# Alternating gate and recurrent projection tiles, one convolution tap a step, in a one-core decoder step

## The chip, the core and the metric

The kernel runs on one core of a Trainium2 chip. A core has a matrix engine (TensorE, here PE, with its weight load PEld), a vector engine (VectorE, here DVE), a scalar engine (ScalarE, here ACT), GpSimd (here POOL) and a queue engine (SyncE, here SP) that starts most DMAs. PE writes to PSUM, in eight banks; DVE and ACT read PSUM and SBUF. Each engine works off its own list of instructions in order, and waits on semaphores where it needs another engine's result. The metric is the device time of one execution in microseconds (us).

## The reference, cut to what matters

The reference is one layer of a decoder on 512 prompt positions and 8 x 4 sample positions (544 columns in all). All in float32.

```
h = RMSNorm_pre(x)
[x_r | q | k | v | g_A | g_B] = h @ W_in                # 1024 -> 4608
A: xc = conv4(x_r) + b;  r, i = sigmoid(block gates of xc)
   a = exp(-8 r softplus(-lam));  h_t = a h_(t-1) + sqrt(1 - a^2) * i * xc
B: attention over a window of 128 (8 query heads, 2 kv heads, sinks, relative bias)
m = (sigmoid(g_A) * (A @ W_A) + sigmoid(g_B) * (B @ W_B)) @ W_out
x = x + RMSNorm_post(m);  then a convolutional feed-forward (1024 -> 8192 -> 1024)
```

`conv4` is a causal convolution of width 4 along the positions, each channel by itself: four products with a scalar per channel, added up.

## The kernel before, in words

Channels lie on the 128 partitions and positions along the free dimension. To keep float32 accuracy, each operand of a matmul is split in a high part (rounded to fp32r, made by ACT with a Copy) and a low part (the rest, made by DVE with a subtraction, which reads the same source and the high part). A product is three matmuls: high by high, high by low, low by high.

**Steps.** The input projection is cut in tiles of 128 output columns. One tile is two calls of `step` (line 342), the first for columns 0 to 255 (matmuls with 256 columns), the second for columns 256 to 543 (288 columns); a step is 24 matmuls over eight blocks of 128 input channels. This text numbers the steps from 0. Steps 0 to 23 are q, k and v. Steps 24 to 39 are the eight tiles of the gate g_B (keys `("in", 28 + c)`, written to `ga`), steps 40 to 55 the eight recurrent tiles x_r (keys `("in", c)`, written to `xr`). Then come steps 56 to 71, the attention output projection (`ao`, matmuls `pmao`), the gate g_A, the recurrent output projection (`lo`) and `out`.

**Ticks.** After the matmuls of step s, `tick` (line 194) sets the clock `now` to s + 1 and writes the other engines' work of that tick in this order: the high parts of the weights of a later tile (ACT, line 281); the `done` function of step s - 1 (list `late`), which reads PSUM; the side jobs that are due (`sides`), in order of their due time; the list `after`; the low parts of the weights (DVE, line 288). So each tick's work stands in this order in the queues of ACT, DVE, POOL and PE, and a tick's work on an engine runs when that engine has come that far. The weights are split two tiles ahead (`look=2`), from step 50 one tile ahead (`look=1`).

**Side jobs.** `attn_unit` is one of 16 units of prompt attention (two heads by 128 positions), begun at the ticks in `ATTN` (8 to 45); each yield passes on to the next tick: scores `psc` on PE; softmax (`s`, `st`) on DVE and ACT; transposes `pt` on PE; split into `tH` (ACT) and `tL` (DVE); the product with V (`pvp`); for every second unit the split of two heads' results into `aH` (ACT, line 840) and `aL` (DVE, line 841). `sample_attn` does the sample positions in two groups (begun at ticks 38 and 43): its transposes `pst` are copied to `spt` by DVE (lines 902 and 903), multiplied in the same tick on PE (`pso`), copied (`so`), transposed (`psot`) and split for eight heads into `aH` (line 921) and `aL` (line 922), 16 columns each, all from one PSUM tile.

**The recurrent branch.** `xr_done` (line 929) scales the projection into the tile `xr`, POOL having written its three leading columns, and after the second half ACT makes the first tap, `xc = xr * w0 + b` (line 943). `xr_taps`, put on the list `after`, adds the other three taps on DVE: each is a scalar_tensor_tensor of 568 columns that reads `xr` and `xc` and writes `xc`. `gates`, due at the ticks in `GATES` (51, 53, 55 and 57 for the first four tiles), splits `xc` (`xcH` on ACT, `xcL` on DVE), multiplies by the block gates (`pg` on PE) a tick later, and takes two sigmoids (`rg`, `ig` on ACT) a tick after that. `lru_exp` (ticks 58 to 61 for the first four) takes tanh and exp on ACT and a square on POOL (line 988). `gate_later` takes the sigmoid of `ga` at ticks 52 to 59. The order of PE, ACT, DVE and POOL in this part is as written; nothing reorders it.

Of the kernel before, what the change touches and what calls it, by code (L numbers as in the profile page):

```python
# [14 lines left out]
ALU = mybir.AluOpType  # L15
# [5 lines left out]
SEQ = 512  # L21
# [8 lines left out]
NH = 8  # L30
# [5 lines left out]
FLAT = SEQ + 7 * DB  # L36
# [42 lines left out]
GATES = (51, 53, 55, 57, 73, 74, 75, 76)  # L79
# [44 lines left out]
def hawk_step(ctx, tc, I, O):  # L124
# [36 lines left out]
    def f32(ap):  # L161
        return ap.bitcast(F32)
# [4 lines left out]
    def sub(out, a, b):  # L167
        dve.tensor_tensor(out=out, in0=a, in1=b, op=ALU.subtract)  # L168
# [7 lines left out]
    def stt(out, a, s_, b, op0, op1):  # L176
        dve.scalar_tensor_tensor(out=out, in0=a, scalar=s_, in1=b, op0=op0, op1=op1)  # L177

    side, now, serial, late, last, mids, after = [], [0], [0], [], [], [], []

    def start_at(t, gen):
        serial[0] += 1
# [9 lines left out]
    def tick(target=0, dt=1):  # L194
        now[0] += dt
        todo = late[:]
        late.clear()
        split = [wsplit_hi(u) for u in wclaim(target)]
        parts_ = [sides, lambda: [f() for f in todo]]
        for f in parts_ if now[0] < TURNED else parts_[::-1]:  # L200
            f()
        for f in after:
            f()
        after.clear()
        for u in split:
            wsplit_lo(*u)
        for f in last:
            f()
        last.clear()
# [23 lines left out]

    qkv_order = (16, 18, 8, 9, 10, 11, 17, 19, 12, 13, 14, 15)
    order = [("in", c) for c in qkv_order]
    order += [("in", 28 + c) for c in range(8)]
    order += [("in", c) for c in range(5)] + [("wg", 0)] + [("in", c) for c in range(5, 8)]
    order += [("ao", c) for c in range(8)] + [("wg", 1)]
    order += [("in", 20 + c) for c in range(8)]
    order += [("lo", c) for c in range(8)]  # L240
# [549 lines left out]
    def attn_unit(hp, n):  # L790
        kv, np_ = hp // 2, n // 2
        nk = 1 if n == 0 else 2
        w = nk * P
        k0 = (n + 1) * P - w
        kh, kl = (K.t[kv][j][:, k0:k0 + w] for j in range(2))
        ps = PX(f"psc{hp}_{n}")
        for j in range(2):
            qh, ql = (Q.t[2 * hp + j][z][:, n * P:(n + 1) * P] for z in range(2))
            o = ps[:, j * w:(j + 1) * w]
            mm(o, qh, kh, True, False)  # L800
            mm(o, ql, kh, False, False)
            mm(o, qh, kl, False, True)
        yield
        s = T(f"s{hp}_{n}")
        s3 = s[:, 0:2 * w].rearrange("p (h j) -> p h j", h=2)
        stt(s3, ps[:, 0:2 * w].rearrange("p (h j) -> p h j", h=2), rq[:, n:n + 1], btab[hp][:, :, 2 * WIN - w:2 * WIN],
            ALU.mult, ALU.add)
        se = softmax_a(s3, 2, sinkb[:, 2 * hp:2 * hp + 2], f"{hp}_{n}")
        yield
        softmax_b(s3, 2, *se)  # L810
        yield
        pt = PX(f"pt{hp}_{n}")
        for ch in range(nk):
            for j in range(2):
                pe.transpose(pt[:, (2 * ch + j) * P:(2 * ch + j + 1) * P], s3[:, j, ch * P:(ch + 1) * P], ident)
        yield
        tH, tL = T(f"tH{hp}_{n}", F32R), T(f"tL{hp}_{n}", F32R)
        act.activation(tH[:, 0:2 * w], pt[:, 0:2 * w], AF.Copy)
        sub(tL[:, 0:2 * w], pt[:, 0:2 * w], f32(tH[:, 0:2 * w]))
        yield  # L820
        if n % 2 == 0:
            pvps[hp] = PX(f"pvp{hp}_{np_}")
        pvp = pvps[hp]
        o = pvp[:, (n % 2) * 256:(n % 2 + 1) * 256]
        for ch in range(nk):
            vh, vl = (V.t[kv][z][:, k0 + ch * P:k0 + (ch + 1) * P] for z in range(2))
            th, tl = (x[:, ch * 256:(ch + 1) * 256] for x in (tH, tL))
            mm(o, vh, th, ch == 0, False)
            mm(o, vl, th, False, False)
            mm(o, vh, tl, False, ch == nk - 1)  # L830
        if n % 2 == 1:
            yield
            for j in range(2):
                hd = 2 * hp + j
                if np_ == 0:
                    A.alloc(hd)
                src = pvp.rearrange("p (n h q) -> p n h q", n=2, h=2)[:, :, j, :]
                oh, ol = (A.get(hd, 0, z) if np_ == 0 else A.t[hd][z][:, 256:512] for z in range(2))
                oh, ol = (x.rearrange("p (n q) -> p n q", n=2) for x in (oh, ol))
                act.activation(oh, src, AF.Copy)  # L840
                sub(ol, src, f32(oh))


# [16 lines left out]
    def sample_attn(g):  # L860
# [54 lines left out]
        pe.transpose(px[:, 0:P], so, ident)  # L915
        yield
        ov = px[:, 0:P].rearrange("p (b h t) -> p b h t", b=4, h=NH)
        for hd in range(NH):
            oh, ol = (A.t[hd][z][:, SEQ + 16 * g:SEQ + 16 * g + 16].rearrange("p (b t) -> p b t", b=4)
                      for z in range(2))  # L920
            act.activation(oh, ov[:, :, hd, :], AF.Copy)
            sub(ol, ov[:, :, hd, :], f32(oh))


# [4 lines left out]
    def xr_done(c, a, ps):  # L929
        if a == 0:  # L930
            xr = xrt[c] = T(f"xr{c}")
            pool.memset(xr[:, 0:3], 0.0)
            pool.tensor_copy(xr[:, SEQ + 3:SEQ + 3 + 7 * DB].rearrange("p (b i) -> p b i", b=DB)[:, :, 0:3],
                             stT[:, c, 0:24].rearrange("p (b i) -> p b i", b=DB))
            scaled(xr[:, 3:259], ps, 0)
            return
        xr = xrt[c]
        smpv = xr[:, SEQ + 3:SEQ + 3 + 7 * DB].rearrange("p (b i) -> p b i", b=DB)
        mul(xr[:, 259:515], ps[:, 0:256], rep[:, 256:512])
        mul(smpv[:, :, 3:7], ps[:, 256:288].rearrange("p (b t) -> p b t", b=DB),  # L940
            rep[:, SEQ:NT].rearrange("p (b t) -> p b t", b=DB))
        xc[c] = S(f"xc{c}")
        act.activation(xc[c][:, 0:FLAT], xr[:, 0:FLAT], AF.Identity, bias=pv[:, C_B + c:C_B + c + 1],
                       scale=pv[:, C_W + c:C_W + c + 1])
        after.append(lambda: xr_taps(c))

    def xr_taps(c):
        xr = xrt[c]
        smpv = xr[:, SEQ + 3:SEQ + 3 + 7 * DB].rearrange("p (b i) -> p b i", b=DB)
        for t in range(1, 4):  # L950
            wv = pv[:, C_W + 8 * t + c:C_W + 8 * t + c + 1]
            stt(xc[c][:, 0:FLAT], xr[:, t:t + FLAT], wv, xc[c][:, 0:FLAT], ALU.mult, ALU.add)
        pool.tensor_copy(stage[:, c, 0:3], xr[:, SEQ:SEQ + 3])
        pool.tensor_copy(stage[:, c, 3:27].rearrange("p (b i) -> p b i", b=DB), smpv[:, :, 4:7])

# [129 lines left out]

    for c in range(8):
        for a in range(2):
            step(("in", 28 + c), h, a, gate_done(sg, c, "ga", True))
        start_at(GATES[0] + c + 1, once(gate_later, sg, c))
    for c in range(8):  # L1090
        for a in range(2):
            step(("in", c), h, a, lambda a, ps, c=c: xr_done(c, a, ps), look=1 if now[0] + 1 >= GATES[0] else 2)

# [874 lines left out]
```

## Time and profile before

| what | value |
|---|---|
| median of 3 runs | 1008.49 us (1007.88 to 1010.76) |
| the profiled execution | 1007.64 us, its span 1005.8 us |
| PE busy in the span | 984.9 us (98%) |
| DVE busy | 750.1 us (75%) |
| ACT busy | 567.8 us (56%) |
| POOL busy | 158.8 us (16%) |
| mean granted PE clock | 0.998 |

The profile is of one execution; its span runs from the first to the last instruction. Lines L12 are lines of the kernel printed above. A row of the timeline gives start, duration, engine, line, operation and the tiles it writes and reads; in brackets the time for which the engine had been idle just before, and the instruction on another engine that ended it. Buffer numbers are left out of the names, so that `xr` stands for all eight tiles.

### The profile page before, as it was taken

How to read it: one execution, taken by the hardware profiler on the slowest of the kernel's cores; microseconds unless marked ns; L12 is line 12 of the kernel's file. 1: busy time of each engine (PE TensorE's matmuls, PEld its weight loads, DVE VectorE, ACT ScalarE, POOL GpSimd, SP SyncE). 2: the span in 40 equal slices, each digit the busy share in tenths (PEclk: the TensorE clock that was granted, in tenths of full speed). 3: DMA queues.
4: the chain of work that ended last, by engine and by line, in shares of the span. 5: the costliest groups of instructions: out<-in, count | busy, mean ns of one | idle time of the engine just before them, and what ended most of it. 6: DMA issues, size and time to landing. Idle time of an engine off the chain costs nothing.

```text
span 1005.8 us, 20110 instructions
## 1 busy us (share of the span) xinstructions
PE 984.9 (98%) x7783; PEld 972.4 (97%) x7783; DVE 750.1 (75%) x1609; ACT 567.8 (56%) x1362; POOL 158.8 (16%) x269
## 2 busy tenths in 40 slices
PE   9999999888999999999999999999999999999997
PEld 8999999888999999999999999999999999999996
DVE  6776666876765854489787687878888888888765
ACT  6544334447749534456776656565656565656652
POOL 2143000000512543020000101111111111111004
PEclk9999999999999999999999999999999999999999
DMA  7665222321332354317235768585858586758612
GB/s 209 174 226 181 75 74 85 96 73 56 91 106 84 93 166 131 110 43 245 74 90 137 178 139 180 139 183 136 187 131 193 124 191 127 189 130 216 195 45 89
DMA packets 211000, 135.62 MB, mean 135 GB/s; under 512 B 8846, under 2 KB 197022, under 8 KB 210873
## 3 DMA queue, kind: packets, MB, share of 16 engines
q1 hardware_dynamic: 198920, 112.72, 39.5%
q0 software_dynamic: 11920, 19.59, 11.8%
q10 hardware_dynamic: 64, 2.04, 0.5%
q8 instruction: 61, 1.00, 0.4%
q14 instruction: 35, 0.28, 0.1%
HBM read 111.78 MB, written 11.37 MB: 122 GB/s over the span
## 4 chain that ended last, share of the span: by engine, by line
PE 88%; DVE 6%; ACT 4%; DMA 1%; issue 1%; SPq 0%; DVEq 0%; ACTq 0%
PE pmin L165 18%; PE pmdn L165 17%; PE pux L1517 15%; PE puy L1517 8%; PE pq L1517 6%; PE pmout L165 5%; PE pmlo L165 5%; PE puz L1517 4%; PE pmao L165 3%; DMA raw_in<-in_w_in_dram 1%; DVE xc L177 1%; PE psc L165 1%; PE pvp L165 1%; PE ptok L165 1%; PE pg L165 1%
## 5 line engine op out<-in xcount | busy, mean ns | idle before, releaser
L165 PE MATMUL pmin<-hH,wh_in 128*128 128x256 f32 (+1 forms) x568 | 165.1, 293 | 0.1
L165 PE MATMUL pmin<-hL,wh_in 128*128 128x256 f32 (+1 forms) x568 | 162.7, 289 | 0.0
L165 PE MATMUL pmin<-hH,wl_in 128*128 128x256 f32 (+1 forms) x568 | 158.9, 288 | 3.1 <-DVE wl_in L288 3.1
L165 PE MATMUL pmdn<-fH,wh_dn 128*128 128x256 f32 (+1 forms) x448 | 129.0, 288 | 0.2 <-DVE ft L174 0.2
L165 PE MATMUL pmdn<-fL,wh_dn 128*128 128x256 f32 (+1 forms) x448 | 128.9, 288 | 0.0
L165 PE MATMUL pmdn<-fH,wl_dn 128*128 128x256 f32 (+1 forms) x448 | 128.9, 288 | 0.0
L177 DVE SCALAR_TENSOR_TENSOR uc<-u,fv,uc 128x560 f32<-128x560 f32 x128 | 102.0, 797 | 13.3 <-ACT uc L1548 13.2
L165 PEld LDWEIGHTS pmin<-hH,wl_in 128*128 128x128 f32 x568 | 105.1, 188 | 3.7 <-DVE wl_in L288 3.5
L165 PEld LDWEIGHTS pmin<-hH,wh_in 128*128 128x128 f32 x568 | 106.9, 188 | 1.6 <-issue 1.2
L165 PEld LDWEIGHTS pmin<-hL,wh_in 128*128 128x128 f32 x568 | 107.1, 189 | 0.1
L165 PEld LDWEIGHTS pmdn<-fH,wh_dn 128*128 128x128 f32 x448 | 84.2, 188 | 0.6 <-issue 0.6
L165 PEld LDWEIGHTS pmdn<-fH,wl_dn 128*128 128x128 f32 x448 | 84.3, 188 | 0.0
L165 PEld LDWEIGHTS pmdn<-fL,wh_dn 128*128 128x128 f32 x448 | 84.2, 188 | 0.0
L1643 ACT COPY u<-pux 128x272 f32<-128x272 f32 x52 | 20.1, 387 | 83.3 <-PE pux L1517 83.3
L168 DVE TENSOR_TENSOR u<-puy,u 128x240 f32<-128x240 f32 (+2 forms) x78 | 24.7, 344 | 49.2 <-PE puy L1517 32.5
L174 DVE TENSOR_TENSOR ft<-ft,pmdn 128x256 f32<-128x256 f32 (+1 forms) x104 | 45.3, 436 | 17.0 <-PE pmdn L165 16.4
L281 ACT ACTIVATE wh_in<-raw_in 128x512 fp32r<-128x512 f32 x70 | 42.5, 626 | 26.8 <-issue 9.8
L1548 ACT ACTIVATE uc<-u,fv 128x560 f32<-128x560 f32 x64 | 48.2, 755 | 0.0
L288 DVE TENSOR_TENSOR wl_in<-raw_in,wh_in 128x512 fp32r<-128x512 f32 x70 | 47.1, 684 | 1.2 <-ACT wh_in L281 1.0
L165 PE MATMUL pmao<-aH,wl_ao 128*128 128x288 f32 (+1 forms) x128 | 37.4, 292 | 2.7 <-DVE wl_ao L288 2.7
L1443 POOL DMA_DIRECT2D raw_up_s<-raw_up_s x26 | 22.7, 872 | 101.5 <-DMA raw_up_s<-raw_up__7496 4.5
L168 DVE TENSOR_TENSOR wl_dn<-raw_dn,wh_dn 128x512 fp32r<-128x512 f32 x56 | 38.4, 686 | 0.0
(779 smaller groups left out, 3395.0 us busy)
## 6 DMA issues: line engine op xcount, KB each, us to landing
raw_in<-in_w_in_dram SPq DMA_DIRECT2D x35, 512.0 KB
raw_dn<-in_w_down_dram SPq DMA_DIRECT2D x56, 256.0 KB
raw_up_s<-in_w_up_dram SPq DMA_DIRECT2D x25, 512.0 KB
raw_up_s<-raw_up_s POOLq DMA_DIRECT2D x26, 256.0 KB, 5.6
raw_ao<-in_w_attn_o_dram SPq DMA_DIRECT2D x8, 512.0 KB
raw_lo<-in_w_lru_o_dram SPq DMA_DIRECT2D x8, 512.0 KB
raw_out<-in_w_out_dram SPq DMA_DIRECT2D x8, 512.0 KB
xdram<-xn POOLq DMA_DIRECT2D x8, 272.0 KB, 8.9
```

The costliest lines, as they stand in the source:

```text
L165: pe.matmul(out, l, r, start=start, stop=stop)
L168: dve.tensor_tensor(out=out, in0=a, in1=b, op=ALU.subtract)
L174: dve.tensor_tensor(out=out, in0=a, in1=b, op=ALU.add)
L177: dve.scalar_tensor_tensor(out=out, in0=a, scalar=s_, in1=b, op0=op0, op1=op1)
L281: act.activation(hl[0], raw, AF.Copy)
L288: (eng or dve).tensor_tensor(out=hl[1], in0=raw, in1=f32(hl[0]), op=ALU.subtract)
L1443: pool.dma_start(out=w["p4"], in_=w["p2"], accum_op=ALU.add)
L1517: pe.matmul(ps[:, :HN], w, x, start=start and k == 0 and i == 0, stop=stop and k == 3 and i == 2, skip_group_check=True)
L1548: act.activation(yt[j][:, 0:FLATU], u[:, 0:FLATU], AF.Copy, scale=fv[:, j:j + 1])
L1643: act.copy(e[nm_], z)
```

## The change

It has three parts.

First, the gate tiles and the recurrent tiles alternate: step 24 + 4c and the next are gate tile c, the two after these recurrent tile c. The order in which the weights are loaded (`order`) changes with it. The gate weights `wg` stay at the same place in it, after 13 tiles. The ticks of the side jobs are the same numbers as before.

Second, the three DVE taps of a recurrent tile are no longer written in one piece on `after`. They go on a list, `taps`, and each tick takes one from it, written directly behind the `done` functions, ahead of the side jobs. The second half of recurrent tile c comes to its `done` at tick 24 + 4c + 5, so its taps stand in the three ticks after that. Before, all three stood at the end of tick 43 + 2c.

Third, in `attn_unit` both high parts are written ahead of both low parts, and in `sample_attn` all eight high parts ahead of the eight low ones, which come one tick later.

```diff
@@ tick
         split = [wsplit_hi(u) for u in wclaim(target)]
-        parts_ = [sides, lambda: [f() for f in todo]]
+        tap = taps[:1]
+        parts_ = [sides, lambda: [f() for f in todo + tap]]
+        del taps[:1]
         for f in parts_ if now[0] < TURNED else parts_[::-1]:
@@ the order of the weights
-    order += [("in", 28 + c) for c in range(8)]
-    order += [("in", c) for c in range(5)] + [("wg", 0)] + [("in", c) for c in range(5, 8)]
+    pairs = [("in", z + c) for c in range(8) for z in (28, 0)]
+    order += pairs[:13] + [("wg", 0)] + pairs[13:]
@@ attn_unit
+            parts_ = []
             for j in range(2):
...
                 act.activation(oh, src, AF.Copy)
+                parts_.append((ol, src, oh))
+            for ol, src, oh in parts_:
                 sub(ol, src, f32(oh))
@@ sample_attn
-        for hd in range(NH):
-            oh, ol = (A.t[hd][z][:, SEQ + 16 * g:SEQ + 16 * g + 16].rearrange("p (b t) -> p b t", b=4)
-                      for z in range(2))
+        parts_ = [[A.t[hd][z][:, SEQ + 16 * g:SEQ + 16 * g + 16].rearrange("p (b t) -> p b t", b=4) for z in range(2)]
+                  for hd in range(NH)]
+        for hd, (oh, ol) in enumerate(parts_):
             act.activation(oh, ov[:, :, hd, :], AF.Copy)
+        yield
+        for hd, (oh, ol) in enumerate(parts_):
             sub(ol, ov[:, :, hd, :], f32(oh))
@@ xr_done and the taps
-        after.append(lambda: xr_taps(c))
+        taps.extend(lambda t=t: xr_tap(c, t) for t in range(1, 4))
 
-    def xr_taps(c):
+    def xr_tap(c, t):
         xr = xrt[c]
+        wv = pv[:, C_W + 8 * t + c:C_W + 8 * t + c + 1]
+        stt(xc[c][:, 0:FLAT], xr[:, t:t + FLAT], wv, xc[c][:, 0:FLAT], ALU.mult, ALU.add)
+        if t < 3:
+            return
         smpv = xr[:, SEQ + 3:SEQ + 3 + 7 * DB].rearrange("p (b i) -> p b i", b=DB)
-        for t in range(1, 4):
-            wv = pv[:, C_W + 8 * t + c:C_W + 8 * t + c + 1]
-            stt(xc[c][:, 0:FLAT], xr[:, t:t + FLAT], wv, xc[c][:, 0:FLAT], ALU.mult, ALU.add)
         pool.tensor_copy(stage[:, c, 0:3], xr[:, SEQ:SEQ + 3])
@@ the steps
     for c in range(8):
         for a in range(2):
-            step(("in", 28 + c), h, a, gate_done(sg, c, "ga", True))
+            step(("in", 28 + c), h, a, gate_done(sg, c, "ga", True), look=1 if now[0] + 1 >= GATES[0] else 2)
         start_at(GATES[0] + c + 1, once(gate_later, sg, c))
-    for c in range(8):
         for a in range(2):
             step(("in", c), h, a, lambda a, ps, c=c: xr_done(c, a, ps), look=1 if now[0] + 1 >= GATES[0] else 2)
```

Three places show how it moves the instructions. The first is DVE's list at ticks 53 to 54, where the `done` of a recurrent tile, the split of `xc` for the gates and the taps meet. Before:

```order
L171 TENSOR_TENSOR xr_3025<-pmin_1_2997,rep 128x8x4
L168 TENSOR_TENSOR xcL_3091<-xc_2615,xcH_3090 128x568
L177 SCALAR_TENSOR_TENSOR xc_3081<-xr_3025,pv,xc_3081 128x568 x3
L288 TENSOR_TENSOR wl_in_3077<-raw_in_2854,wh_in_3076 128x512
L171 TENSOR_TENSOR xr_3130<-pmin_0_3049,rep 128x256
```

Now (with the line numbers of the changed kernel):

```order
L171 TENSOR_TENSOR xr_3032<-pmin_1_3004,rep 128x8x4
L168 TENSOR_TENSOR xcL_3101<-xc_2035,xcH_3100 128x568
L290 TENSOR_TENSOR wl_in_3087<-raw_in_2874,wh_in_3086 128x512
L171 TENSOR_TENSOR ga_3135<-pmin_0_3059,rep 128x256
L177 SCALAR_TENSOR_TENSOR xc_3091<-xr_3032,pv,xc_3091 128x568
L171 TENSOR_TENSOR xc_1855<-ig_3095,xc_1855 128x568
```

The three taps stood between the wait for `xcH` and the weights' low part `wl_in`; now the first of them stands behind that low part and behind the next `done`.

The second place is DVE's list at ticks 31 and 32, in the stretch that held gate tiles alone, with a unit of attention beside them. Before:

```order
L171 TENSOR_TENSOR ga_1889<-pmin_1_1861,rep 128x288
L168 TENSOR_TENSOR tL_1_1936<-pt_1_1891,tH_1_1935 128x512
L177 SCALAR_TENSOR_TENSOR s_2_1939<-psc_2_1896,rq,btab_1089 128x512
...
L288 TENSOR_TENSOR wl_in_1932<-raw_in_1749,wh_in_1931 128x512
L171 TENSOR_TENSOR ga_1978<-pmin_0_1904,rep 128x256
L174 TENSOR_TENSOR st_2_1941<-st_2_1941 128x2
```

Now:

```order
L171 TENSOR_TENSOR ga_1894<-pmin_1_1866,rep 128x288
L177 SCALAR_TENSOR_TENSOR xc_1855<-xr_1800,pv,xc_1855 128x568
L168 TENSOR_TENSOR tL_1_1943<-pt_1_1897,tH_1_1942 128x512
L177 SCALAR_TENSOR_TENSOR s_2_1946<-psc_2_1902,rq,btab_1089 128x512
...
L290 TENSOR_TENSOR wl_in_1938<-raw_in_1749,wh_in_1937 128x512
L171 TENSOR_TENSOR xr_1985<-pmin_0_1910,rep 128x256
L177 SCALAR_TENSOR_TENSOR xc_1855<-xr_1800,pv,xc_1855 128x568
L174 TENSOR_TENSOR st_2_1948<-st_2_1948 128x2
```

A tap has come in ahead of the attention's work of each of the two ticks.

The third place is ACT's list at tick 49, the split of the sample group's result, with what each instruction waits for. Before:

```order
L818 ACTIVATE tH_3_2863<-pt_3_2812 128x512 [waits PE_49]
L921 ACTIVATE aH_1151<-psot_2817 128x16 [waits PE_49]
L921 ACTIVATE aH_1155<-psot_2817 128x16 [waits DVE_49]
L921 ACTIVATE aH_1605<-psot_2817 128x16 [waits DVE_49]
...
L281 ACTIVATE wh_in_2917<-raw_in_2608 128x512 [waits Activation_49]
```

Now:

```order
L820 ACTIVATE tH_3_2883<-pt_3_2832 128x512 [waits PE_49]
L926 ACTIVATE aH_1151<-psot_2837 128x16 [waits PE_49]
L926 ACTIVATE aH_1154<-psot_2837 128x16
L926 ACTIVATE aH_1605<-psot_2837 128x16
...
L283 ACTIVATE wh_in_2924<-raw_in_2638 128x512 [waits Activation_49]
```

Each high part after the first waited for the low part before it; now none waits for DVE. The order of PE's and SP's instructions is the same in kind as before, with gate and recurrent tiles exchanged.

More of the change, by code (lines that the diff above doesn't have):

```diff
@@ L177, in stt @@
         dve.scalar_tensor_tensor(out=out, in0=a, scalar=s_, in1=b, op0=op0, op1=op1)
-    side, now, serial, late, last, mids, after = [], [0], [0], [], [], [], []
+    side, now, serial, late, last, mids, after, taps = [], [0], [0], [], [], [], [], []
     def start_at(t, gen):
```

## The prediction

> **What bounds the kernel now.** I read the page first: busy times and the slices.
>
> ```profile
> PE 984.9 (98%) x7783; PEld 972.4 (97%) x7783; DVE 750.1 (75%) x1609; ACT 567.8 (56%) x1362; POOL 158.8 (16%) x269
> PE   9999999888999999999999999999999999999997
> PEclk9999999999999999999999999999999999999999
> ```
>
> PE is the bound: it lacks 1005.8 - 984.9 = 20.9 us of the span, at the start, at the end and in the slices with an 8, near 175 to 250 us. That is where the diff works. The view by stretches cuts it at step 24 (107.5), the end of step 41 (169.6), the end of step 55 (234.9) and the middle of step 60 (257.9).
>
> ```profile
> core 0: us, PE busy (x) PEld busy (x) DVE busy (x) ACT busy (x) POOL busy (x), PEclk, DMA share, GB/s
> 107.50:169.60 62.10, 62.10 (x503) 62.10 (x503) 37.58 (x103) 22.56 (x60) 0.26 (x2) 1.00 0.30 85
> 169.60:234.90 65.30, 57.08 (x477) 54.47 (x476) 46.47 (x118) 31.65 (x78) 3.64 (x28) 1.00 0.26 78
> 234.90:257.90 23.00, 19.50 (x146) 18.39 (x145) 17.24 (x29) 19.07 (x30) 2.79 (x6) 1.00 0.17 51
> 257.90:300.00 42.10, 42.10 (x335) 41.90 (x333) 28.60 (x47) 22.48 (x40) 14.84 (x24) 1.00 0.38 111
> ```
>
> With the gate tiles PE has no gap and DVE has room (38 of 62 us). With the recurrent tiles PE loses 65.30 - 57.08 = 8.22 us, then 23.00 - 19.50 = 3.50 us in the first ao steps, 11.72 in all, and nothing after. No change to the order here can win more than these gaps and what it costs to start again behind them. The view of waits for PE from 140 to 300 us says for whom PE waits:
>
> ```profile
> PE pso L165 <- DVE spt L903: 4.0, 2, 2.5
> PE pmin L165 <- DVE wl_in L288: 3.1, 2, 1.7
> PE pmao L165 <- DVE wl_ao L288: 2.7, 4, 0.9
> PE pkc L874 <- DVE aL L168: 1.1, 1, 1.1
> PE pmao L165 <- ACT wh_ao L281: 0.8, 1, 0.8
> ```
>
> All but 0.8 us is DVE, which is busy only 71% of 169.6 to 234.9. So it is late, not full: its queue stands still for ACT, and long work stands ahead of what PE needs.
>
> What a gap costs beyond its length: a step of 24 matmuls with 256 columns takes 165.95 - 163.04 = 2.91 us from its first matmul to the next instruction; one with a gap of 1.39 us takes 231.53 - 227.03 = 4.50. That is 1.59, 0.20 more than the gap.
>
> ```profile
> 163.04 0.36 PE L165 MATMUL pmin<-hH,wh_in 128*128 128x256 f32 x1
> 165.95 0.28 PE L165 MATMUL pvp<-tH,vH 128*128 128x256 f32 x1
> 227.03 0.28 PE L165 MATMUL pmin<-hH,wh_in 128*128 128x256 f32 x1
> 230.24 0.38 PE L165 MATMUL pmin<-hH,wl_in 128*128 128x256 f32 x1 [1.39 <-DVE wl_in L288]
> 231.53 0.30 PE L165 MATMUL pmin<-hH,wh_in 128*128 128x288 f32 x1
> ...
> 234.71 0.29 PE L165 MATMUL pg<-xcH,wh_wg 128*128 128x284 f32 x1
> ...
> 236.29 0.27 PE L165 MATMUL pmao<-aH,wh_ao 128*128 128x256 f32 x1
> ...
> 255.72 0.38 PE L165 MATMUL pmao<-aH,wh_ao 128*128 128x256 f32 x1 [0.80 <-ACT wh_ao L281]
> ...
> 256.45 0.39 PE L165 MATMUL pmao<-aH,wl_ao 128*128 128x256 f32 x1 [0.23 <-DVE wl_ao L288]
> ```
>
> The rows after it give, from start to start, 234.71 - 231.53 = 3.18 us for a step with 288 columns and 236.29 - 234.71 = 1.58 for the 12 matmuls of `pg`.
>
> **The taps.** The groups of DVE's work and its timeline give:
>
> ```profile
> L177 DVE SCALAR_TENSOR_TENSOR xc<-xr,pv,xc 128x568 f32<-128x568 f32 x24 | 19.4, 808 | 1.3 <-ACT xc L943 0.8
> ...
> 205.89 2.49 DVE L177 SCALAR_TENSOR_TENSOR xc<-xr,pv,xc 128x568 f32<-128x568 f32 x3
> ...
> 233.72 0.75 DVE L168 TENSOR_TENSOR xcL<-xc,xcH 128x568 fp32r<-128x568 f32 x1 [3.11 <-ACT xcH L958]
> ...
> 242.62 0.75 DVE L168 TENSOR_TENSOR xcL<-xc,xcH 128x568 fp32r<-128x568 f32 x1 [3.10 <-ACT xcH L958]
> ```
>
> No tap is added or removed: 24 of 0.81 us. Counted by ticks, the 24 now run 21 in ticks 43 to 55 and 3 in tick 57; after the change 10 run in ticks 30 to 42, 11 in 43 to 56 and 3 in 58 to 60. So 10 x 0.81 = 8.1 us of DVE work leave the second stretch for the first. DVE's load becomes 37.6 + 8.1 = 45.7 of 62.1 us (74%) in the first, 46.5 - 8.1 = 38.4 in the second, where PE's own work is 57.1 (67%). What covers the ten taps in the first stretch is DVE's 24.5 us of idle time there; if that cover were gone, they would cost up to 8.1 us.
>
> The average hides the order within a tick. From 233.72 to 242.62 DVE needs 8.9 us for two ticks: 3.1 waiting for `xcH`, the split, three taps (2.4), `wl`, and the next tick. PE needs 2.91 + 3.18 + 1.58 = 7.7 in the same time, so it loses about 1.2 per pair; that is the 1.39 at 230.24 and the gaps for `wl_ao` behind it. Without the three taps ahead of `wl`, and with one tap elsewhere in the pair, DVE needs 8.9 - 2.4 + 0.8 = 7.3, under PE's 7.7. Every second pair also loses the 0.8 of ACT's first tap in its wait, since a recurrent tile is done every four ticks. The `wl_in` and `wl_ao` gaps should close. The gap at `pkc` and the two before `pso` come from DVE being behind at ticks 45, 46 and 51, each a tick or so behind three taps; they should close too, but at tick 46 a tap is now ahead of the copy that `pso` awaits, so I leave some of it.
>
> **High parts first.** The timelines of DVE and ACT show the alternation, and what eight small operations take in a row:
>
> ```profile
> 182.84 0.43 DVE L168 TENSOR_TENSOR aL<-pvp,aH 128x256 fp32r<-128x256 f32 x1 [1.26 <-ACT aH L840]
> 183.72 0.42 DVE L168 TENSOR_TENSOR aL<-pvp,aH 128x256 fp32r<-128x256 f32 x1 [0.45 <-ACT aH L840]
> ...
> 202.14 0.17 DVE L168 TENSOR_TENSOR aL<-psot,aH 128x16 fp32r<-128x16 f32 x1
> 202.56 0.17 DVE L168 TENSOR_TENSOR aL<-psot,aH 128x16 fp32r<-128x16 f32 x1 [0.25 <-ACT aH L921]
> ...
> 205.11 0.17 DVE L168 TENSOR_TENSOR aL<-psot,aH 128x16 fp32r<-128x16 f32 x1 [0.25 <-ACT aH L921]
> ```
> ```profile
> 202.77 0.19 ACT L921 ACTIVATE aH<-psot 128x16 fp32r<-128x16 f32 x1 [0.24 <-DVE aL L168]
> ```
> ```profile
> 150.64 0.90 DVE L171 TENSOR_TENSOR qs<-qs,rep 128x32 f32<-128x32 f32 x8
> ```
>
> A sample group holds DVE from 202.14 to 205.28, 3.1 us, and ACT as long; eight in a row take about 0.9, so 2.2 us of DVE's queue go, twice, at ticks 49 and 54. They stand a tick later, ahead of `wl`. For a pair of heads the first low part starts one high part later (about 0.3) and the second 0.45 earlier: little, eight times. None of it is on PE; it is slack for the gaps above, and I add nothing for it. The added wait is that of the first low part for all high parts; behind it stand `wl` and the next `done`, which PE needs two steps later at the earliest.
>
> **What ACT then holds back.** From tick 57 ACT works without a pause:
>
> ```profile
> 239.61 0.87 ACT L943 ACTIVATE xc<-xr,pv 128x568 f32<-128x568 f32 x1 [3.79 <-DVE xr L171]
> 244.33 1.28 ACT L986 ACT_TABLE_LOAD   x1
> ...
> 255.03 1.68 ACT L281 ACTIVATE wh_ao<-raw_ao 128x512 fp32r<-128x512 f32 x3
> ```
>
> It needs 255.03 - 239.61 = 15.4 us from the last recurrent tile's first tap to the weights for step 60, and the change leaves that chain as it is. Now it starts 4.7 us after step 55 ended at 234.9, because DVE was late with `xr`. With DVE in time it starts 0.5 us after that end, so the weights come at about 15.9 + 0.5, their low part at 17.1. Before, PE got there at 255.72 - 0.80 = 254.9, 20.0 after that end, with three of the four `wl_ao` gaps on the way (2.7 less the 0.23 at 256.45, so 2.5); without them and 0.2 for each, at 16.9. So a gap of 0.2 remains, between nothing and 1; with starting again 0.5. DMA stands apart: the weights' order and their number per step are the same, at a DMA share of 0.26 to 0.30.
>
> **The sum.** 11.72 + 10 gaps x 0.2 = 13.7 us at most. Less 0.5 for step 60, and 1.5 for what may stay at tick 46 and elsewhere (an allowance: a third of the 4.0 us before `pso`), 11.7 are won. The profiled execution took 1007.64, 1.84 over its span, and becomes 995.9; the median of the runs stands 0.85 higher, so I predict 996.8.
>
> **Rivals.** First, ACT takes over at ticks 57 to 60. If its chain starts no earlier than now relative to step 55, because the sigmoids wait for `pg` or `xr` comes late after all, the gap at step 60 grows by the 4.2 us that I let it gain: 1001.0. ACT's 19.07 busy us in 23.0 speak for it, its 3.79 us of idle time just before the chain against it: 14%.
>
> Second, DVE and POOL get in each other's way. The taps of the last tile move from tick 57 to ticks 58 to 60, where POOL squares:
>
> ```profile
> 237.74 0.74 DVE L171 TENSOR_TENSOR xc<-ig,xc 128x568 f32<-128x568 f32 x1
> ...
> 246.63 1.58 DVE L171 TENSOR_TENSOR xc<-ig,xc 128x568 f32<-128x568 f32 x1
> ```
> ```profile
> 246.48 1.13 POOL L988 TENSOR_TENSOR lt<-rg 128x568 f32<-128x568 f32 x1 [6.67 <-ACT rg L986]
> ```
>
> The same DVE operation took 0.74 alone and 1.58 beside POOL's. Three taps stretched by 0.84 each, all ahead of a `wl_ao` that PE awaits, would give 996.8 + 2.5 = 999.3. I give it 5%, since at tick 60 DVE waits for ACT anyhow. [...]
>
> Third, slower: DVE becomes the bound in the first stretch. A tap stands ahead of `tL` and the softmax in ticks 30 to 42, and PE's transposes need them two steps on. It decides if DVE's work with its waits for ACT passes PE's 62.1 / 18 = 3.45 us per tick. All ten taps would then fall on PE, 8.1 us, and the second stretch would hand over part of its gaps: with half of the 11.7 won, 996.8 + 5.9 + 8.1 = 1010.8. Against it: 45.7 us of 62.1, and two steps of lead. 7%.
>
> Fourth, no change: PE's waits are put down to DVE but end on something that stays, such as a buffer or the order of PE's own list; 1008.5, 4%. That leaves 70% for the forecast.
>
> **Range and chances.** A change under 0.3% (3 us) can't be told from none in this kernel. From below, all gaps closed give 994.8; runs of before lie 0.6 under and 2.3 over their median, so I take 993.5. From above, the first two rivals are taken in with some of both: 1003.5. That leaves out the third and fourth, and a tail. Faster: 70 + 14 + 5, of which I give 1 away: 0.88; same 0.04; slower 0.08.
>
> **What would show it.** Right: PE's waits for `spt`, `wl_in` and `aL` between 160 and 250 us gone or under 1 us in sum; DVE about 74% busy with PE unbroken before; ACT's waits for `aL` gone; one remaining wait of PE near step 60. Wrong: PE waiting for `pt` or `pvp` between 120 and 170 us, or several microseconds for `wh_ao` at steps 58 to 60.

## The result and the profile after

The changed kernel took 995.14 us (median of 4 runs, 994.97 to 995.54), the kernel before 1009.57 (1007.88 to 1010.76). The ratio is 0.9859, with a 95% interval of 0.9841 to 0.9877: 1.4% faster. The forecast was 996.8, its range 993.5 to 1003.5. The profiled execution took 994.97 us, its span 993.2.

The page of the changed kernel, busy times and slices of PE:

```profile
span 993.2 us, 20120 instructions
...
PE 983.9 (99%) x7783; PEld 972.7 (98%) x7783; DVE 746.6 (75%) x1609; ACT 566.5 (57%) x1362; POOL 160.4 (16%) x269
...
PE   9999999999999999999999999999999999999997
```

PE does the same work as before (983.9 us against 984.9), and the three slices with an 8 are gone. The span is 12.6 us shorter, and all of that is PE's idle time and what follows it.

The view by stretches of the changed kernel, cut at the same places of the program (the end of step 24, the end of step 41, the end of step 55, the middle of step 60):

```profile
107.60:169.70 62.10, 62.10 (x503) 62.10 (x503) 44.15 (x117) 24.55 (x61) 2.84 (x16) 1.00 0.27 78
169.70:225.90 56.20, 56.20 (x477) 54.30 (x476) 40.90 (x110) 28.39 (x75) 1.68 (x12) 1.00 0.32 94
225.90:244.80 18.90, 18.50 (x145) 18.10 (x145) 12.77 (x22) 18.11 (x28) 3.60 (x6) 1.00 0.20 58
```

The number behind the bounds of a row is its length, the next PE's busy time; the number behind the last bracket is the granted clock. The second stretch, 65.30 us before, has no gap at all now; the third, 23.00 before, has 0.40 left. PE's waits from 140 to 300 us say which:

```profile
PE pmao L165 <- DVE wl_ao L290: 0.2, 1, 0.2
PE pmao L165 <- ACT wh_ao L283: 0.2, 1, 0.2
```

These two, at step 60, are what is left of the 11.72 us in ten gaps of before. The starts of PE's steps give where the time went. The table compares a step's length, from its first matmul to that of the next step, in both traces.

| step | length before, us | after | won | gaps of before in it |
|---|---|---|---|---|
| 44 | 6.35 | 5.08 | 1.27 | 1.09 at `pkc`, for `aL` |
| 45 | 6.89 | 4.36 | 2.53 | 2.48 at `pso`, for `spt` |
| 50 | 7.61 | 3.98 | 3.63 | 1.70 for `wl_in`, 1.56 for `spt` |
| 54 | 4.50 | 2.82 | 1.68 | 1.39 for `wl_in` |
| 56 | 4.13 | 2.81 | 1.32 | 0.87 for `wl_ao` |
| 58 | 4.97 | 2.83 | 2.14 | 0.85 and 0.75 for `wl_ao` |
| 60 | 4.41 | 3.75 | 0.66 | 0.80 for `wh_ao`, 0.23 for `wl_ao`; 0.40 stays |

No other step from 24 to 71 differs by more than 0.1 us. In sum 13.2 us: 11.3 of gaps that are gone, and 1.9 for starting again behind the eight that closed, 0.24 for each on average (0.05 in step 45, 0.45 in step 56). Outside these steps the two profiled executions differ by 0.6 the other way (0.1 ahead of step 24, 0.1 over the other steps up to 71, 0.4 behind them), without a wait of PE that would explain it; so 12.6 are left.

DVE's timeline shows the third part of the change, and the wait for ACT that stayed:

```profile
200.81 0.73 DVE L168 TENSOR_TENSOR aL<-psot,aH 128x16 fp32r<-128x16 f32 x8
...
214.30 0.75 DVE L168 TENSOR_TENSOR xcL<-xc,xcH 128x568 fp32r<-128x568 f32 x1 [3.10 <-ACT xcH L966]
214.97 0.69 DVE L290 TENSOR_TENSOR wl_in<-raw_in,wh_in 128x512 fp32r<-128x512 f32 x1
```

The eight low parts of a sample group take 0.73 us in a row, where the group held DVE for 3.1. DVE still waits 3.10 us for `xcH`, but `wl_in` now follows directly. The three taps that stood between them are gone from there, and nobody waits.

### The profile page after: what moved, and what is told of

Read it like the earlier page. It is cut to its first block, busy times and chain, and to the rows that moved or that the text cites. A ratio compares the mean times of both kernels' runs of the same rounds, so it can differ in the third digit from the quotient of the medians.

```text
span 993.2 us, 20120 instructions
## 1 busy us (share of the span) xinstructions
PE 983.9 (99%) x7783; PEld 972.7 (98%) x7783; DVE 746.6 (75%) x1609; ACT 566.5 (57%) x1362; POOL 160.4 (16%) x269
## 4 chain that ended last, share of the span: by engine, by line
PE 93%; ACT 2%; DVE 2%; DMA 1%; issue 0%; SPq 0%; DVEq 0%; ACTq 0%
PE pmin L165 21%; PE pmdn L165 17%; PE pux L1524 16%; PE puy L1524 8%; PE pq L1524 6%; PE pmout L165 5%; PE pmlo L165 5%; PE puz L1524 4%; PE pmao L165 4%; DMA raw_in<-in_w_in_dram 1%; PE psc L165 1%; PE pvp L165 1%; PE pg L165 1%; PE ptok L165 1%; PE pt L817 1%
## 5 line engine op out<-in xcount | busy, mean ns | idle before, releaser
L177 DVE SCALAR_TENSOR_TENSOR uc<-u,fv,uc 128x560 f32<-128x560 f32 x128 | 102.0, 797 | 13.3 <-ACT uc L1555 13.2
L283 ACT ACTIVATE wh_in<-raw_in 128x512 fp32r<-128x512 f32 x70 | 42.8, 628 | 29.8 <-issue 12.1
L174 DVE TENSOR_TENSOR ft<-ft,pmdn 128x256 f32<-128x256 f32 (+1 forms) x104 | 45.2, 436 | 17.1 <-PE pmdn L165 16.6
L168 DVE TENSOR_TENSOR wl_dn<-raw_dn,wh_dn 128x512 fp32r<-128x512 f32 x56 | 38.4, 685 | 0.0
L165 PE MATMUL pmout<-mH,wh_out 128*128 128x272 f32 x128 | 37.4, 292 | 0.0
```

Source lines behind the costliest of these rows:

```text
L165: pe.matmul(out, l, r, start=start, stop=stop)
L174: dve.tensor_tensor(out=out, in0=a, in1=b, op=ALU.add)
L283: act.activation(hl[0], raw, AF.Copy)
```

## The experiments

### The three parts one by one

The first three kernels make one part of the change alone, on top of the kernel before. First the alternating order:

```diff
-    order += [("in", 28 + c) for c in range(8)]
-    order += [("in", c) for c in range(5)] + [("wg", 0)] + [("in", c) for c in range(5, 8)]
+    pairs = [("in", z + c) for c in range(8) for z in (28, 0)]
+    order += pairs[:13] + [("wg", 0)] + pairs[13:]
...
         start_at(GATES[0] + c + 1, once(gate_later, sg, c))
-    for c in range(8):
```

> The kernel before with the alternating tile order alone; the three taps stay in one piece at the end of the tick, low parts stay behind each high part. Theory (DVE is late where three taps and the alternation stand ahead of what PE awaits): the lumps now come every four ticks instead of every two, 8 us of taps leave the crowded stretch, and only the gap before the second sample product, where a lump and the sample group's alternation still meet, stays with about 2 us: 11 us faster than before, near 998. Rival (the high parts first carry the gain): less than 4 us faster. Rival (the spread of the taps carries it): less than 4 us faster.

Measured: 998.35 us (998.10 to 998.81), ratio 0.9890 (0.9869 to 0.9912). PE's waits of this run:

```profile
PE pmin L165 <- DVE wl_in L288: 2.9, 2, 1.7
PE pso L165 <- DVE spt L903: 0.7, 2, 0.5
```

The order alone closes the gaps for `wl_ao` but for 0.2 us, and most of those before `pso`. What it does not close are two waits for `wl_in`, which end at 205.35 and 224.95. I had expected about 2 us to stay, but at the second `pso`. DVE's timeline shows what stands ahead of `wl_in` there:

```profile
201.42 0.17 DVE L168 TENSOR_TENSOR aL<-psot,aH 128x16 fp32r<-128x16 f32 x1 [0.25 <-ACT aH L921]
...
202.20 2.50 DVE L177 SCALAR_TENSOR_TENSOR xc<-xr,pv,xc 128x568 f32<-128x568 f32 x3
204.61 0.68 DVE L288 TENSOR_TENSOR wl_in<-raw_in,wh_in 128x512 fp32r<-128x512 f32 x1
...
223.47 0.17 DVE L168 TENSOR_TENSOR aL<-psot,aH 128x16 fp32r<-128x16 f32 x1 [0.25 <-ACT aH L921]
223.56 0.74 DVE L171 TENSOR_TENSOR xc<-ig,xc 128x568 f32<-128x568 f32 x1
224.22 0.68 DVE L288 TENSOR_TENSOR wl_in<-raw_in,wh_in 128x512 fp32r<-128x512 f32 x1
```

The rows of `aL` are each the last of a sample group's eight, which alternate with ACT for 3.1 us. They stand ahead of both waits, with three taps in one piece behind them the first time and ahead of them the second.

Then the taps alone. Without the alternating order a recurrent tile is done every second tick, so two taps are taken in a tick:

```diff
+        tap = taps[:2]
-        parts_ = [sides, lambda: [f() for f in todo]]
+        parts_ = [sides, lambda: [f() for f in todo + tap]]
+        del taps[:2]
```

> The kernel before with the taps spread alone: tile order as before, at most two taps per tick (a recurrent tile is done every second tick, so one per tick would fall behind), placed behind the done functions. Theory: DVE's total in the recurrent stretch stays, only the taps now run while DVE would wait for ACT and the weights' low part comes earlier; about half the gaps close: 5 us faster than before, near 1004. Rival (the order within the tick is everything): 10 us or more faster.

Measured: 1005.98 us (1003.15 to 1007.52, 10 runs), ratio 0.9961 (0.9947 to 0.9976). PE's waits:

```profile
PE pso L165 <- DVE spt L905: 3.7, 2, 2.1
PE pmao L165 <- ACT wh_ao L283: 2.5, 1, 2.5
PE pmin L165 <- DVE wl_in L290: 0.8, 2, 0.4
```

The waits for the weights' low parts shrink, but two taps now stand ahead of `spt` at tick 46, and the wait for ACT at step 60 grows from 0.8 to 2.5 us: counted from the end of step 55, PE gets there 2.5 us sooner, while ACT's chain starts only 0.9 sooner. This is nearly my first rival, in a kernel that is not the changed one. I had expected half of the gaps to close; 7.8 us of the 11.72 stay.

Last, the high parts first, alone (as in the diff of the change):

> The kernel before with the high parts ahead of the low ones alone. Theory: it takes 2.2 us from DVE's queue at ticks 49 and 54, which shortens the gaps behind them (1.7 and 1.4 us) and part of the rest: 4 us faster than before, near 1005. Rival (this part carries the gain): 9 us or more faster.

Measured: 1003.84 us (1001.63 to 1004.25), ratio 0.9939 (0.9918 to 0.9960). `wl_in` is no longer waited for, though the three taps still stand in one piece; 3.4 us for `spt` stay, as does most of `wl_ao`:

```profile
PE pso L165 <- DVE spt L906: 3.4, 2, 2.5
PE pmao L165 <- DVE wl_ao L288: 1.8, 3, 0.8
```

### Two parts together

The changed kernel without the third part, and then without the second (the taps in one piece at the end of a tick, as before):

> The changed kernel with the low parts put back behind each high part. Theory: the high parts first are only slack; without them DVE is 1.5 to 2 us later at ticks 49 to 51 and 54 and PE may wait up to 1 us for the second sample product: 995 to 997. Rival (the high parts first carry the gain): 1000 or more.

> The changed kernel with the three taps of a tile put back in one piece at the end of the tick. Theory: with the lumps four ticks apart and the high parts first, DVE catches up between lumps and PE waits under 1 us in all: 995 to 996.5. Rival (the spread is what closes the gaps): 1000 or more.

The first took 996.12 us (995.93 to 996.26), ratio 0.9867 (0.9849 to 0.9885), the second 995.21 (994.89 to 995.56), ratio 0.9861 (0.9836 to 0.9885). Without the third part PE waits once for `spt`, and longer at step 60:

```profile
PE pso L165 <- DVE spt L905: 1.2, 1, 1.2
PE pmao L165 <- ACT wh_ao L283: 0.7, 1, 0.7
```

So the third part is worth 1.0 us on top of the others, and spreading the taps nothing that can be measured. Then the second and the third part without the alternating order:

> The kernel before with the taps spread (at most two per tick) and the high parts first, without the alternating order. Theory: DVE's work in the recurrent stretch is 46 us less 4 us of waiting against 57 us on PE, so most gaps close, with 2 to 4 us left at the pairs of ticks that hold three taps and the gates' split: 997 to 1000. Rival (without the alternation DVE stays the bound): 1003 or more.

Measured: 996.68 us (996.57 to 999.08), ratio 0.9880 (0.9856 to 0.9903), just under the range that I expected, with 1.6 us for `spt` and 1.0 for `wh_ao` left. All eight combinations side by side, with the lowest time beside the median, because some of these kernels scatter (the last section shows why):

| parts | median, us | lowest |
|---|---|---|
| none (the kernel before, 23 executions) | 1009.55 | 1007.11 |
| order | 998.35 | 998.10 |
| taps | 1005.98 | 1003.15 |
| high parts | 1003.84 | 1001.63 |
| order, taps | 996.12 | 995.93 |
| order, high parts | 995.21 | 994.89 |
| taps, high parts | 996.68 | 996.57 |
| all three | 995.14 | 994.97 |

By the lowest times the parts alone win 9.0, 4.0 and 5.5 us, 18.5 in sum; together they win 12.1. They are substitutes: each gives DVE slack at the same few places, and any two leave PE only 0.6 to 2.8 us of waits out of 11.72.

### Is DVE full or late?

The changed kernel with one spare reduction on DVE in each of ticks 29 to 56, used by nothing:

```diff
+        if 29 <= now[0] <= 56:
+            for _ in range(1):
+                dve.tensor_reduce(spare, rep, AX.X, ALU.max)
         for f in after:
```

> The changed kernel with one more DVE operation in each tick from 29 to 56, a reduction of 544 columns of 0.7 us that nobody waits for: 28 x 0.7 = 20 us more DVE work in 116 us of PE work. Theory (DVE's busy time of about 84 us and its waits for ACT of about 15 leave it some 15 us short of PE): the room is used up and 2 to 6 us come through: 997 to 1001. Rival (DVE is not what PE waits for): no change, 995. Rival (DVE was at its bound already in the changed kernel): 10 us or more slower, 1005 and above.

Measured: 996.13 us (995.53 to 996.69), ratio 0.9868 (0.9847 to 0.9890). The group of these reductions, and the one new wait of PE:

```profile
L206 DVE TENSOR_REDUCE spare<-rep 128x1 f32<-128x544 f32 x28 | 19.9, 712 | 0.0
```
```profile
PE pso L165 <- DVE spt L912: 1.1, 1, 1.1
```

19.9 us more work on DVE cost 1.0 us, less than the 2 to 6 that I expected. Then with two a tick:

> Edit: the changed kernel, with two spare reductions of 544 columns on DVE in each of the ticks 29 to 56, ahead of what stands last in the tick; the spare result is used by nothing. By the profile of the run with one such reduction each takes 0.71 us, so this is 56 x 0.71 = 40 us of DVE work where one a tick was 20. In the changed kernel DVE is busy 44.2 of 62.1 us in the stretch from step 24 to the end of step 41 and 41.4 of 56.8 us in that to the end of step 55, 85.6 in 118.9 together. Theory (DVE was late in single places, not full, and the slack of each tick covers work up to a threshold): with one reduction a tick 105 of 119 us still nearly fits; with two DVE needs 125.5 us and, with some 12 us of waits for ACT, 137, more than PE's 119, so DVE becomes the bound, PE waits some 15 us for it in many places and the time is near 1010 (1004 to 1015). Rival (DVE's total load plays no part, only the places of single instructions): at most one or two microseconds over the run with one reduction, 996 to 998.

Measured: 1014.64 us (1014.12 to 1016.60, 7 runs), ratio 1.0049 (1.0032 to 1.0067), slower than the kernel before. PE's waits:

```profile
PE pt L821 <- DVE s L786: 4.8, 3, 2.2
PE pmao L165 <- ACT wh_ao L286: 2.9, 1, 2.9
PE pkc L883 <- DVE aL L168: 1.9, 1, 1.9
PE pmin L165 <- DVE wl_in L293: 1.7, 2, 1.3
PE pso L165 <- DVE spt L912: 1.5, 2, 0.8
```

The next 20 us cost 18.5. There is a threshold between them, as the theory had it, but the waits shown here and the smaller ones come to only 13.5 us. The rest I put down to starting again and to a lower granted clock (0.50 in three stretches of 3.41 us, in the last section). The first wait, for the softmax's `s` at `pt`, is the one that my third rival named, and 2.2 us of it lie in the first stretch: it comes, but with 40 us more work, not with the 6.6 that the first stretch got.

### What is left at step 60

The sigmoids of the last two gate tiles stand at ticks 58 and 59, between tanh and exp on ACT. Here they are made at tick 57, beside the others:

```diff
-        start_at(GATES[0] + c + 1, once(gate_later, sg, c))
+        start_at(min(GATES[0] + c + 1, 57), once(gate_later, sg, c))
```

> The changed kernel with the sigmoids of the gate tiles 6 and 7 moved from ticks 58 and 59 to tick 57, so that ACT loads its tables three times instead of five at ticks 58 to 60, 2.6 us less on the chain that ends at step 60. Theory: the two gaps left at step 60 (0.17 and 0.23 us, and the start behind each) close, 0.5 to 0.8 us faster than the changed kernel, near 994.5. Rival (the room on ACT lets nothing else come earlier, or the weights' high part behind the two sigmoids comes late at step 58): no change or up to 1 us slower.

Measured: 993.52 us (993.21 to 993.68), ratio 0.9842 (0.9822 to 0.9863): 1.6 us under the changed kernel, and so faster than both kernels. In the trace of the changed kernel ACT loads a function table, in 1.28 us, ahead of exp and again ahead of the sigmoid behind it (at 231.28, 233.36, 236.51 and 238.60 us). Its loads in that kernel, for exp (L994) and the sigmoid of `ga` (L1091):

```profile
L994 ACT ACT_TABLE_LOAD x5 | 6.4, 1283 | 0.1
L1091 ACT ACT_TABLE_LOAD x3 | 3.8, 1283 | 0.1
```

and with the sigmoids earlier:

```profile
L994 ACT ACT_TABLE_LOAD x4 | 5.1, 1283 | 0.1
...
L1091 ACT ACT_TABLE_LOAD x2 | 2.6, 1283 | 0.0
```

Two loads of 1.28 us leave the chain ahead of step 60, which takes 239.04 - 226.33 = 12.7 us in place of 15.4, and PE has no wait left from 140 to 300 us. By the starts of the steps, step 60 is 0.92 us shorter: 0.40 of gaps and 0.52 for starting again behind them, a little over the 0.5 to 0.8 that I expected. Another 0.3 is won in steps 63 to 65, without a wait in the trace there, and 0.2 ahead of step 24, which is no work of the edit. So about 0.9 of the 1.6 us is shown to be the edit's.

Is the spread of the taps worth something once this wait is gone? The same edit with the taps in one piece:

> Edit: as the changed kernel, but with the three taps of a tile in one piece at the end of the tick, as before the change, and with the sigmoids of the last two gate tiles at tick 57. It asks whether spreading the taps is worth anything once ACT's chain at step 60 no longer hides it. Without the earlier sigmoids the two forms took 995.21 (in one piece) and 995.14 (spread). Theory (with gate and recurrent tiles in turn a tick with three taps has a tick without any behind it, and DVE's slack covers the lump): the same as the run with the earlier sigmoids and spread taps, 993.5, within 0.5, with at most a wait of 0.2 us for spt. Rival (the spread is what keeps DVE in time, and the wait for ACT covered that up): a wait for wl_ao or spt appears and the time is 994.5 or more.

Measured: 993.76 us (993.38 to 994.12), ratio 0.9840 (0.9815 to 0.9864). It isn't: 0.24 us, inside the scatter of either, and one wait of 0.2 for `spt`.

### Why the kernel before scatters

Executions of the kernel before differ by 5 us, with the mean granted clock. To see whether PE's idle time does that, spare matmuls fill it in the kernel before, without making it shorter. They write a tile that the next product overwrites:

```diff
+    def fill(ps, n):
+        x = h.get(0, 0, 0)
+        for _ in range(n):
+            mm(ps[:, 0:256], x[:, 0:P], x[:, 0:256], True, True)
...
         po = PX(f"pso{g}")
+        fill(po, 20 if g == 0 else 12)
```

> Edit: the kernel before, with 20 spare matmuls of 256 columns on PE right ahead of the first product of pso and 12 ahead of the second, into the tile that the product then overwrites; PE waits there 2.48 and 1.56 us in the kernel before, and at 0.12 us each the spare ones fill 2.4 and 1.4 us of it without making it longer. Question: executions of the kernel before differ, 1007.2 to 1007.7 us at a mean granted clock of 0.998 to 1.000, about 1010.3 at 0.996 and about 1012 at 0.993, and in three profiles of experiments the granted clock is 0.50 for about 3 us behind the wait for spt. Theory (the granted clock falls because PE stands idle there): with the idle time filled the clock behind the first pso stays whole, most executions lie at 1007.0 to 1007.8 with a clock of 0.998 or more, and the median falls from about 1010.3 to below 1009. Rival (the clock falls for something else, or for the pso products themselves): the executions scatter as before, median 1010 or more.

and further, in `step`:

```diff
+        if key in (("in", 5), ("in", 7)) and a == 0:
+            fill(ps, 13 if key[1] == 5 else 11)
```

> Edit: as the run with spare matmuls ahead of pso, and also 13 spare matmuls ahead of step 50 and 11 ahead of step 54, in which PE waits 1.70 and 1.39 us for wl_in; they take 1.5 and 1.3 us, of the time that it would wait later in the step. Theory (idle time of PE sets the granted clock): no execution with a clock under 0.998, all within 1007.0 to 1008.0, median near 1007.4, though no term of the work that PE waits for has changed. Rival: scatter up to 1012 as before.

Measured: 1007.58 us (1007.23 to 1008.01, 12 runs), ratio 0.9981 (0.9971 to 0.9990), and 1007.50 (1007.33 to 1008.04, 12 runs), ratio 0.9984 (0.9974 to 0.9994). The kernel before took 1009.55 beside them (1007.11 to 1012.31, 23 runs). The timeline of PE in the first of the two shows the filling:

```profile
188.20 2.65 PE L165 MATMUL pso<-hH 128*128 128x256 f32 x20
190.78 0.48 PE L165 MATMUL pso<-vnt,spt 64*128 64x128 f32 x2
```

| executions | mean granted clock | time, us |
|---|---|---|
| before, 8 of 23 | 0.998 to 1.000 | 1007.1 to 1007.8 |
| before, 2 of 23 | 0.998 | 1009.1 and 1009.6 |
| before, 11 of 23 | 0.995 to 0.997 | 1008.6 to 1010.8 |
| before, 2 of 23 | 0.993 | 1011.5 and 1012.3 |
| spare matmuls, 24 of 24 | 0.998 to 1.000 | 1007.2 to 1008.0 |

32 matmuls more, on the engine that bounds the kernel, take 2.0 us off its median. What PE awaits comes no earlier (`pso` starts at 190.78 us here and at 190.59 in the profile of before); only the clock stayed whole (1.00 from 186 to 194 us). The second kernel adds nothing to the first: filling the two waits before `pso` is enough. The mean clock does not set the two executions at 0.998 and 1009 us apart: it also holds the last microseconds of an execution, behind PE's last matmul, and there the clock is 0.50 (3.7 us in the profile of before, from 1002.09, and 4.0 in that of the changed kernel, from 989.13).

## Why the prediction was right, point by point

**What bounds the kernel.** Right. PE's gaps were 11.72 us, 11.3 of them are gone, and its work did not change.

**What a gap costs beyond its length.** I took 0.20 from one pair of steps; the table of steps gives 0.24 over eight, and 0.26 at step 60 from the run with earlier sigmoids. Right on average, though one pair could not show it: step 54, from which I took it, gives 0.29 against itself after the change (2.82 us, where the step that I compared it with took 2.91).

**The taps.** The count is right: ten taps in the first stretch, 8.03 us of DVE's work on the tile `xc` in the trace after:

```profile
107.50:169.60 62.10, 8.03 (x10) 1.00 0.27 79
```

DVE's load there came to 44.2 us (71%) for the 45.7 that I worked out, and in the second stretch to 40.9 of 56.2 (73%) for 38.4 of 57.1. I had carried the taps over by ticks and left the rest as it stood. But DVE had been late before: two of the 21 taps, two low parts `wl_ao` and one product of `xc` ran behind the end of step 55 and now run ahead of it, some 3.7 us by their rows. Rows directly behind each other overlap by about 0.1 us (214.30 and 214.97 above), so the busy time of a filled stretch grows by less than its rows. The cover held in both. But what I credited to the taps is not theirs: the order and the high parts close the same gaps without the spread, 995.21 us against 995.14. The working from 233.72 to 242.62 holds for `wl_ao`, which the order alone all but closes. It does not hold for the two waits for `wl_in`, the 1.39 at 230.24 among them: a sample group's eight pairs, 3.1 us, stand ahead of both (in the kernel before from 202.14 and from 225.78), and the working left them out. With the high parts first and nothing else, these waits are gone; with the order alone they stay at 2.9 us. Spreading the taps closes them only together with the order; alone it leaves 0.8.

**High parts first.** I set it at nothing on PE and called it slack for the gaps above. On top of the other two parts it is 1.0 us; alone it is 5.5 by the lowest times. The price of DVE's wait (3.1 to about 0.9 us for eight) was measured as 0.73. The sentence that it adds nothing held only because the sum counted every gap as closed already. That the forecast named the taps for a gain that the high parts bring as well, and still met the time, is luck in this sense: the change held both.

**The allowance.** This is the term of the sum that was mis-sized. I left 1.5 us for the tap ahead of `spt` at tick 46. `pso` does not wait in the changed kernel; it waits 1.2 with order and taps without the third part, and that at tick 51, behind the alternation for a pair of heads, not behind the tap at tick 46. The right figure was nothing.

**Step 60.** ACT's chain was forecast at 15.4 us, starting 0.5 after the end of step 55:

```profile
226.56 0.86 ACT L950 ACTIVATE xc<-xr,pv 128x568 f32<-128x568 f32 x1 [1.66 <-DVE xr L171]
...
241.97 1.68 ACT L283 ACTIVATE wh_ao<-raw_ao 128x512 fp32r<-128x512 f32 x3
```

It takes 241.97 - 226.56 = 15.41, and the wait for it is there, as PE's timeline shows:

```profile
242.67 0.38 PE L165 MATMUL pmao<-aH,wh_ao 128*128 128x256 f32 x1 [0.17 <-ACT wh_ao L283]
...
243.40 0.39 PE L165 MATMUL pmao<-aH,wl_ao 128*128 128x256 f32 x1 [0.23 <-DVE wl_ao L290]
```

I gave a gap of 0.2, with starting again 0.5. It is 0.40 in two pieces, and 0.92 with starting again behind both. Step 55 ends at 225.9; PE is there 242.50 - 225.9 = 16.6 us later, 0.3 sooner than I had worked out, and the chain starts 0.7 us after that end instead of 0.5. So PE waits for the high part too, which I had ready in time, and pays for a second start.

**The sum.** 13.7 at most less 0.5 was 13.2, which is what the steps show; two small misses cancel in it, gaps of 11.3 for 11.5 and 1.9 for 1.7 for starting again. Of that 0.6 was lost outside the change, and the allowance of 1.5 was too much: 0.9 us in the profiled execution, 994.97 for 995.9. The other 0.7 of the 1.7 us by which the median fell below the forecast is the offset from profile to median. I carried the 0.85 of the kernel before over, and it is 0.17 after. The profile of before was one of the executions with a whole clock. Most of the others took 1 to 5 us more at a lower mean clock, which the spare matmuls take away, and of the gaps the changed kernel has only 0.40 us.

**The rivals.** ACT taking over at ticks 57 to 60 did not come in this kernel (0.40 us), but in part it did with the taps alone (2.5). DVE against POOL: one tap shows it in DVE's timeline,

```profile
233.91 1.25 DVE L177 SCALAR_TENSOR_TENSOR xc<-xr,pv,xc 128x568 f32<-128x568 f32 x1
...
238.28 0.80 DVE L177 SCALAR_TENSOR_TENSOR xc<-xr,pv,xc 128x568 f32<-128x568 f32 x1
```

beside POOL's square from 233.43 to 234.57: 0.45 us more, of the 0.66 that were left of the square, and nobody waits for it. The row of the prediction lost 0.84 of the 0.98 us that were left of its square. So in both rows DVE's operation took longer beside the square, by less than the rest of it. DVE as the bound in the first stretch fell: PE is unbroken from 107.6 to 169.7, and one spare reduction a tick brings no wait there either. (107.5 is the end of step 24, not its start, so the stretch holds 17 steps of 3.65 us and not 18 of 3.45; the argument stands.)

## What to carry to other kernels

Where an in-order engine is 71% busy and yet waited for, look at what stands between a long wait of its queue and the instruction that the bounding engine needs. Several edits then win the same microseconds, so price them together and not one by one. In a median, count a gap of the bounding engine dearer than its length: beyond starting again (0.24 us for each gap here) it can lower the engine's clock behind it (to 0.50 for 3.41 us here). Where a chain of another engine ends a wait by a few tenths, look for function-table loads that a different order saves (here two of 1.28 us).

## What the runs showed of the hardware that I had not expected

PE's granted clock fell from 1.00 to 0.50 behind some of its gaps. By stretches, the kernel with the taps alone, whose PE waited 1.63 us until 188.30:

```profile
186.69:190.10 3.41, 1.80 (x25) 1.00 0.06 15
190.10:193.52 3.42, 3.42 (x19) 0.50 1.04 285
193.52:196.93 3.41, 3.41 (x31) 1.00 0.05 13
```

The column behind the counts is the granted clock. It is 0.50 for 3.41 us, then whole again; matmuls with 256 columns start 0.21 us apart instead of 0.12, and step 46 takes 6.02 us from its start to the next, for 4.48 in the kernel before. The kernel with the high parts alone shows the same behind 2.48 us at the same place:

```profile
187.25:190.67 3.42, 0.94 (x8) 1.00 0.21 62
190.67:194.08 3.41, 3.41 (x28) 0.50 0.54 151
```

and the kernel with two spare reductions a tick three times, behind waits of 1.95, 1.94 and 2.94 us:

```profile
187.44:190.85 3.41, 3.41 (x17) 0.50 0.00 0
...
194.26:197.68 3.42, 3.42 (x16) 0.50 0.52 156
...
262.53:265.94 3.41, 3.41 (x17) 0.50 0.80 228
```

The profiled execution of before had the wait of 2.48 us as well, and a whole clock behind it:

```profile
186.31:189.72 3.41, 1.81 (x14) 1.00 0.48 145
189.72:193.14 3.42, 2.54 (x31) 1.00 0.19 51
```

So behind the same gap the clock halved in one profile and not in the other. That PE's idle time does it is what the spare matmuls show: with them the mean clock was 0.998 or more in 24 executions of 24, without them in 10 of 23.

What decides in the single case was not shown. The three stretches at 0.50 in the kernel with two spare reductions begin 6.82 and 75.09 us apart, 2 and 22 times 3.413 us (75.09 / 22). The rows of before are cut at such distances from 1002.09 us, where the clock falls in that trace. The wait, from 188.12 to 190.59, lies across two of them, with 1.81 and 2.54 us of PE's work; with the high parts alone the wait, from 187.98 to 190.46, lies in the one stretch ahead of the halving, with 0.94. But PE's busy time alone does not draw the line: with the taps alone a stretch with 1.80 us of work lost the clock, and in the profile of before one with 1.71, from 206.79 to 210.20, kept it (1.00 up to 213.61).
